# Attention probabilities and the residual turned by VectorE blocks and DMA instead of TensorE transposes

## The chip, the cores and the metric

One core of one Trainium2 chip runs the kernel. The time is the device time of one execution in microseconds (us), the median of the runs shown. TensorE (PE in the profile) multiplies matrices into eight accumulator banks; VectorE (DVE) and ScalarE (ACT) do the elementwise work, GpSimd (POOL) nearly nothing here. SyncE (SP) issues all the DMAs that this text speaks of, from one queue of its own.

## What is computed

Two layers of a transformer over 512 tokens of width 1,024, in float32: a state-space mixer (SSD), then latent attention (MLA) with 16 heads, each mixer behind a root-mean-square norm and added to the residual `h`, and a last norm. The change lies in the second layer. Cut to that:

```python
def mla_mixer(u, positions, in_w, q_norm_w, kv_norm_w, uq_w, ukv_w, out_w):
    proj = u @ in_w                                   # c_q 384, c_kv 256, k_r 64, z 2048
    q = rms_norm(c_q, q_norm_w) @ uq_w                # 16 heads x (128 + 64)
    kv = rms_norm(c_kv, kv_norm_w) @ ukv_w            # 16 heads x (128 + 128): k_nope, v
    q_full = [q_nope, rope(q_rope)]; k_full = [k_nope, rope(k_r)]
    o = causal_block_attention(q_full, k_full, v, 192 ** -0.5)
    return (o * silu(z)) @ out_w

def attend(qb, bi):                                   # a block of 128 queries
    s = einsum('bqhd,bkhd->bhqk', qb, k) * scale
    s = where(key_pos <= q_pos, s, -inf)
    return einsum('bhqk,bkhd->bqhd', softmax(s), v)
...
h = h + mla_mixer(rms_norm(h, norm_w[1]), ...)
return rms_norm(h, final_norm_w)
```

## The kernel before

**Precision.** A float32 operand is split in an upper half (ScalarE casts it to the matmul's float32 form) and a lower half (VectorE subtracts that from the operand), and each product is three matmul passes: upper by upper, upper by lower, lower by upper. So each weight and each activation costs a ScalarE cast and a VectorE subtraction before TensorE can use it. `split_weight` does it for weights (L272 and L273), `split` for activations (L311, L312). `weight()` keeps one unit split ahead of the one in use and one more loaded: loads go into 2 buffers (`raw`), halves into 3 (`whi`, `wlo`). `gemm` (L291) is a projection; it yields every six matmuls, so that other work can be placed between.

**Orders.** TensorE runs its instructions in the order in which the code is written. The order on the other engines, and that of SP's DMAs, is made by the scheduler of the framework from the same program; each engine then runs its list strictly from front to back.

**Stages.** The SSD layer lasts until about 415 us. Then come six projections of the MLA layer (U_M1, 24 matmuls each). In between, the residual, held as eight tiles of 128 channels by 512 tokens, is turned to tokens by channels: 32 TensorE transposes (L682), four to a bank, eight ScalarE copies and eight DMAs (L686) into a DRAM tile `hd`, from which the output projection reads it back at the end. Then come the norms, the first head's projections, and the head loop (L886 to L905), which runs from about 510 to 777 us:

- An even turn of the loop (h even) projects for head h+2, from weight `ua`: first the rope part of q for heads h+2 and h+3, rotated in `rope` (L687 to L701) with the help of four DMAs that swap row groups (L697), three VectorE passes (L698 to L700), and split into `s1` and `s2` (L736 to L739); then q (split by L311, L312) and k (L721 to L723) of head h+2.
- An odd turn projects q and k of head h+2 from weight `ub`, and the values of heads h+1 and h+2 from `uc` (L774).
- Each of the first eleven turns adds one projection of the gate (`zgemm`, weight `w`, result `z` at L712); later ones have pieces of the output projection (`out_tok`).

Into this feed go the steps of the attention, placed by hand-written tables of shares of the turn's cost: SC for `score(h+1, b)`, TU for `turn(h, kb)`, PR for `product(h, kb)`; SF places the scores of head 0 ahead of the loop.

- `score` (L794 to L799): block b of 128 queries against 128 (b+1) keys; then mask and maximum in one VectorE pass (L806; block 0 has a pass more, L804), the exponential on ScalarE (L223), reciprocal (L808) and scaling (L809) on VectorE. The probabilities `p` stand with queries on the partitions.
- `turn` (L818): TensorE transposes, 10 a head, bring them to keys on the partitions in a bank `pt`; ScalarE's cast makes `ph` (L822), VectorE's subtraction `pl` (L823).
- `product` (L836): three matmuls per key block into `po`; after the last, VectorE multiplies by the gate (L838).

A loop turn h thus holds the projections for head h+2, the scores of head h+1, and the transposes and products of head h. What the prediction calls an even head is an even turn of this loop.

Of the kernel before, what the change touches and what calls it, by code (L numbers as in the profile page):

```python
# [15 lines left out]
P = 128  # L16
T = 512
# [22 lines left out]
P1 = (1.0, 2.4, 3.8, 12.0, 18.2)  # L40
GN = 16.84
G7 = 33.0
SF = (0.02, 0.1, 2.1, 3.1)
SC = (0.0, 0.16, 0.25, 0.44)
TU = (0.02, 0.08, 0.38, 0.55)
PR = (0.3, 0.48, 0.65, 0.94)
KO = (3, 4, 5, 8, 10)
# [104 lines left out]
class Net:  # L152
# [497 lines left out]
    def mla(self):  # L650
# [5 lines left out]
        nc.sync.dma_start(con[:], t["con"][:, K_MASK:])  # L656
        self.mask, self.cosT, self.sinT = con[:, 0:T], con[:, T:2 * T], con[:, 2 * T:3 * T]
        hd = self.dram.tile([NCH, P, D], F32, name="hd")
        vh, vl = [], []
        for k in range(KD):  # L660
            h = self.h[k]
# [8 lines left out]
        for i in range(6):  # L670
            w = self.weight("w", U_M1 + i)
            ps = self.bank("mm")
            self.run(self.gemm(ps[:], w, vh, vl, KD))
            if i == NU:
                pss = self.sumsq([h[:] for h in self.h], D, "b")
                r1 = self.rstd_of(pss, D)
            if i >= 2:
                c = i - 2
                for n in range(2):
                    pt = self.bank("pt")  # L680
                    for k in range(4):
                        nc.tensor.transpose(pt[:, k * P:(k + 1) * P], self.h[4 * n + k][:, c * P:(c + 1) * P],  # L682
                                            self.ident)
                    ht = wk.tile([P, T], F32, tag=("ph", "pl")[n], name=self.nm("ht"))
                    nc.scalar.copy(ht[:], pt[:])
                    nc.sync.dma_start(hd[c, :, n * T:(n + 1) * T], ht[:])  # L686
            pend.append(ps)  # L687
            while pend and i >= NU:
                o = self.o16.tile([P, T], F32, tag="o", name=self.nm("cq"))
                v.tensor_tensor(o[:], pend.pop(0)[:], r1[:], op=ALU.mult)  # L690
                cq.append(o)
# [87 lines left out]
                f["v"].append((va, vb))  # L779
                yield 1.3  # L780

        probs = [[] for _ in range(MH)]

        def score(h, b):
            f, i = F[h // 2], h % 2
# [21 lines left out]
            self.E(p[:], p[:], AF.Exp, scale=-1.0, bias=st[:, 0:1], accum_out=st[:, 1:2])  # L807
            v.reciprocal(st[:, 2:3], st[:, 1:2])  # L808
            v.tensor_scalar(p[:], p[:], st[:, 2:3], None, op0=ALU.mult)  # L809
            probs[h].append(p)  # L810

        parts, acc = [[] for _ in range(MH)], {}

        def turn(h, kb):
            n = T - kb * P
            pt = self.bank("pt")
            for b in range(kb, NCH):
                nc.tensor.transpose(pt[:, (b - kb) * P:(b - kb + 1) * P], probs[h][b][:, kb * P:(kb + 1) * P],  # L818
                                    self.ident)
            ph = wk.tile([P, T], F32R, tag="ph", name=self.nm("ph"))  # L820
            pl = wk.tile([P, T], F32R, tag="pl", name=self.nm("pl"))
            nc.scalar.copy(ph[:, :n], pt[:, :n])  # L822
            v.tensor_tensor(pl[:, :n], pt[:, :n], ph[:, :n].bitcast(F32), op=ALU.subtract)  # L823
            parts[h].append((ph, pl))

        def product(h, kb):
# [20 lines left out]
            yield from self.out_tok(zt, 0, hd)  # L847

        def norm(tiles, n, cw):
            at = (wk, ("qh", "ql", "s2") if n == KVL else ("ph", "pl", "s2"))  # L850
            pss = self.sumsq([x[:] for x in tiles], n, "b", *at)
            r = self.rstd_of(pss, n, *at)
            hs, ls = [], []
            for i, x in enumerate(tiles):
                v.scalar_tensor_tensor(x[:], x[:], col(cw + i), r[:], op0=ALU.mult, op1=ALU.mult)
                a = wk.tile([P, T], F32R, tag="ch", name=self.nm("ch"), bufs=5)
                b = wk.tile([P, T], F32R, tag="cl", name=self.nm("cl"), bufs=5)
                nc.scalar.copy(a[:], x[:])
                v.tensor_tensor(b[:], x[:], a[:].bitcast(F32), op=ALU.subtract)
                hs.append(a)  # L860
                ls.append(b)
            return hs, ls

        outg = out0()
        self.run(zgemm(0))
# [15 lines left out]
        self.run(zgemm(3))  # L881
        zsilu(0)
        self.run(fa)
        self.run(front_b(0))
        self.sched(zgemm(4), [(x, functools.partial(score, 0, b)) for b, x in enumerate(SF)])
        for h in range(MH):  # L886
            if h and h % 4 == 0:
                zsilu(h // 4)
            feed, cost = [], 0.0
            j = h // 2 + 1  # L890
            if h < 14:
                feed.append(front_a(j) if h % 2 == 0 else front_b(j))
                cost += 5.2 if h % 2 == 0 else 5.9
            if h < 11:
                feed.append(zgemm(5 + h))
                cost += 5.2
            if h >= 11:
                k = KO[h - 11]
                feed.append(itertools.islice(outg, k))
                cost += 1.3 * k  # L900
            at = SC if h + 1 < MH else ()
            pieces = [(x * cost, functools.partial(score, h + 1, b)) for b, x in enumerate(at)]
            pieces += [(x * cost, functools.partial(turn, h, b)) for b, x in enumerate(TU)]
            pieces += [(x * cost, functools.partial(product, h, b)) for b, x in enumerate(PR)]
            self.sched(chain(*feed), pieces)  # L905
# [166 lines left out]
```

## Time and profile before

| | before |
|---|---|
| median of the runs | 840.74 us (840.42, 840.74, 841.0) |
| the profiled execution's own time | 840.15 us |
| its span, first to last instruction | 838.3 us |
| TensorE's granted clock over the span | 0.998 |
| TensorE busy (weight loads beside it) | 822.8 us, 98% (694.8) |
| VectorE / ScalarE / GpSimd busy | 640.2 (76%) / 453.5 (54%) / 0.2 us |
| DRAM read / written | 83.12 / 4.33 MB |

The profile's busy row gives each engine's busy time, its share of the span and its instructions; PEld is TensorE's loading of weights, which overlaps its matmuls. The chain of waits goes back from the last instruction to what released it, and names the share of the span that each engine holds. A row of it has the start, the length, and the engine, tile and line; "x9" is nine instructions in a row. A row of a group has the line, engine, operation, output and inputs with their shapes, and the count; then busy us and the mean ns of one; then the idle time just ahead of them and what ended it. An arrow `<-` after a number names what ended a wait. Line numbers are those of the kernel before, unless the kernel after is named; there, lines behind the residual's block stand one to fifteen off.

### The profile page before, as it was taken

To read this page: it belongs to the slowest core of one execution; us is meant where nothing else is said; L and a number is where in the kernel's file an instruction comes from. 1 tells how busy PE (TensorE), PEld (TensorE's weight loads), DVE (VectorE), ACT (ScalarE), POOL (GpSimd) and SP (SyncE) were. 2 spreads that over 40 slices of the span, in tenths; PEclk is the share of its full clock that TensorE was granted. 3 is DMA by queue.
4 is the path that set the end of the run, shared out by engine and by line. 5 is a ranking of instruction groups with operands and counts; after the bars stand their busy time and mean duration, and the time that the engine had idled before them with its cause. 6 is when DMAs were issued, how large, how long until landed. Compare 5 with 4: busy or idle time off the path is not lost.

```text
span 838.3 us, 11586 instructions
## 1 busy us (share of the span) xinstructions
PE 822.8 (98%) x4260; PEld 694.8 (83%) x4260; DVE 640.2 (76%) x1226; ACT 453.5 (54%) x802; POOL 0.2 (0%) x4
## 2 busy tenths in 40 slices
PE   7999999999999999999999999999999999999996
PEld 5887888888888888888888888888888888888885
DVE  7899898979788979776564887786767869675544
ACT  7567755545565657333354664456547557554233
POOL 0000000000000000000000000000000000000000
PEclk9999999999999999999999999999999999999999
DMA  6354543434242424323225242222221224331212
GB/s 227 102 186 145 153 150 106 147 101 128 98 151 76 151 87 137 121 95 101 90 86 176 79 129 64 77 65 73 73 64 56 89 75 157 100 100 53 92 59 100
DMA packets 35112, 90.55 MB, mean 108 GB/s; under 512 B 4784, under 2 KB 6320, under 8 KB 35056
## 3 DMA queue, kind: packets, MB, share of 16 engines
q1 hardware_dynamic: 34336, 88.77, 32.9%
q10 hardware_dynamic: 720, 1.05, 0.3%
q8 instruction: 33, 0.54, 0.3%
q14 instruction: 23, 0.19, 0.1%
HBM read 83.12 MB, written 4.33 MB: 104 GB/s over the span
## 4 chain that ended last, share of the span: by engine, by line
PE 91%; DVE 5%; DMA 2%; ACT 1%; issue 1%; SPq 0%; DVEq 0%; ACTq 0%
PE mm L291 54%; PE ot L942 11%; PE s L794 5%; PE mm L300 4%; PE po L836 4%; PE mm L774 3%; PE pt L818 2%; PE yd L138 2%; PE yd L291 1%; PE aux L130 1%; PE aux L105 1%; DMA x<-in_x_dram 1%; PE aux L77 1%; PE aux L89 1%; DMA L<-ac_d 1%; DVE wlo L273 1%
## 5 line engine op out<-in xcount | busy, mean ns | idle before, releaser
L272 ACT CAST whi<-raw 128x1024 fp32r<-128x1024 f32 (+3 forms) x132 | 127.0, 965 | 214.7 <-PE mm L291 177.4
L273 DVE TENSOR_TENSOR wlo<-raw,whi 128x1024 fp32r<-128x1024 f32 (+3 forms) x132 | 146.8, 1115 | 56.1 <-ACT whi L272 55.8
L291 PE MATMUL mm<-ah,whi 128*128 128x512 f32 x384 | 153.9, 401 | 0.0
L291 PE MATMUL mm<-ah,wlo 128*128 128x512 f32 x384 | 150.1, 391 | 0.4 <-DVE wlo L273 0.4
L291 PE MATMUL mm<-al,whi 128*128 128x512 f32 x384 | 149.8, 390 | 0.0
L291 PE MATMUL mm<-vh,whi 128*128 128x512 f32 x224 | 89.6, 400 | 0.9 <-ACT whi L272 0.9
L291 PE MATMUL mm<-vh,wlo 128*128 128x512 f32 x224 | 87.8, 392 | 0.7 <-DVE wlo L273 0.7
L291 PE MATMUL mm<-vl,whi 128*128 128x512 f32 x224 | 87.5, 391 | 0.0
L291 PEld LDWEIGHTS mm<-ah,wlo 128*128 128x128 f32 x384 | 72.1, 188 | 16.0 <-DVE wlo L273 0.8
L291 PEld LDWEIGHTS mm<-ah,whi 128*128 128x128 f32 x384 | 72.2, 188 | 15.5 <-issue 1.4
L291 PEld LDWEIGHTS mm<-al,whi 128*128 128x128 f32 x384 | 72.2, 188 | 14.4 <-DVE al L312 0.3
L942 PE MATMUL ot<-whi,ah 128*128 128x512 f32 (+1 forms) x136 | 52.3, 384 | 0.0
L942 PE MATMUL ot<-whi,al 128*128 128x512 f32 (+1 forms) x136 | 51.4, 378 | 0.0
L942 PE MATMUL ot<-wlo,ah 128*128 128x512 f32 (+1 forms) x136 | 51.4, 378 | 0.0
L291 PEld LDWEIGHTS mm<-vh,wlo 128*128 128x128 f32 x224 | 42.0, 188 | 10.8 <-DVE wlo L273 1.5
L291 PEld LDWEIGHTS mm<-vh,whi 128*128 128x128 f32 x224 | 42.1, 188 | 9.2 <-ACT whi L272 1.1
L223 ACT ACTIVATE p<-p,st 128x128 f32<-128x128 f32 (+1 forms) x64 | 36.1, 564 | 25.1 <-DVE st L806 25.0
L291 PEld LDWEIGHTS mm<-vl,whi 128*128 128x128 f32 x224 | 42.2, 188 | 7.2
L822 ACT CAST ph<-pt 128x512 fp32r<-128x512 f32 (+1 forms) x64 | 26.5, 422 | 33.2 <-PE pt L818 32.8
L291 PE MATMUL mm<-ch,whi 128*128 128x512 f32 x104 | 42.6, 409 | 0.0
L291 PE MATMUL mm<-ch,wlo 128*128 128x512 f32 x104 | 40.8, 392 | 0.0
L291 PE MATMUL mm<-cl,whi 128*128 128x512 f32 x104 | 40.7, 392 | 0.0
(225 smaller groups left out, 1642.6 us busy)
## 6 DMA issues: line engine op xcount, KB each, us to landing
raw<-in_w_dram SPq DMA_DIRECT2D x100, 512.0 KB, 3.3
L<-ac_d SPq DMA_DIRECT2D x32, 256.0 KB, 3.8
E<-ea_d SPq DMA_DIRECT2D x32, 128.0 KB, 3.3
raw<-in_ua_dram SPq DMA_DIRECT2D x8, 512.0 KB, 3.3
raw<-in_ub_dram SPq DMA_DIRECT2D x8, 320.0 KB, 2.9
x<-in_x_dram SPq DMA_DIRECT2D x8, 256.0 KB, 4.3
res<-in_x_dram SPq DMA_DIRECT2D x8, 256.0 KB, 3.3
hd<-ht SPq DMA_DIRECT2D x8, 256.0 KB, 2.3
```

The source lines that it names most:

```text
L138: nc.tensor.matmul(yd[64 * h:64 * h + 64, s], self.xdt[j][:, c, h, :], self.L[2 * j + h][:, s], start=True, stop=True)
L223: i = self.nc.scalar.activation(out, in_, func, **k)
L272: nc.scalar.copy(hi[:, a:b], raw[:, a:b])
L273: nc.vector.tensor_tensor(lo[:, a:b], raw[:, a:b], hi[:, a:b].bitcast(F32), op=ALU.subtract)
L291: self.nc.tensor.matmul(ps, a, b, start=i == 0, stop=i == len(seq) - 1)
L300: self.nc.tensor.matmul(p, seq[i][0], seq[i][1], start=i == 0, stop=i == 3 * ks - 1)
L774: nc.tensor.matmul(ps[:, c2 * 256:(c2 + 1) * 256], a, b, start=i == 0, stop=i == 5)
L794: nc.tensor.matmul(ps[:, :n], x[:, s], y[:, :n], start=k == 0, stop=k == 4)
L818: nc.tensor.transpose(pt[:, (b - kb) * P:(b - kb + 1) * P], probs[h][b][:, kb * P:(kb + 1) * P], self.ident)
L822: nc.scalar.copy(ph[:, :n], pt[:, :n])
L836: nc.tensor.matmul(po[:, kb * P:], x, y, start=kb == 0 and k == 0, stop=kb == NCH - 1 and k == 2)
L942: nc.tensor.matmul(ps[:, a:b], x, y, start=start and i == 0, stop=stop and i == 5)
```

## The change

Both transposes leave TensorE.

- *Residual.* VectorE's `transpose`, which turns each 32x32 block in its place, is applied to each of the eight residual tiles (two in each of the last four of the six projections; L681 of the kernel after); four DMAs a tile (L684), one for each group of 32 partitions, put the blocks in their turned places in `hd`, in runs of 32 numbers (128 bytes).
- *Probabilities.* At the end of each `score`, VectorE turns the 32x32 blocks of `p` into a tile `pb` (L810; two buffers), and four DMAs on SP (L814) write them to a DRAM tile `pd`, one for even and one for odd heads, again in runs of 128 bytes. A new piece, `fetch(h)`, stands right behind the four scores of the head, as the fifth entry of SC and SF: four DMAs (L830) read the key blocks back, whole rows, into tiles `pl`: for even heads four tiles of their own, for odd heads four tiles (`sqa`, `r0`, `rt`, `sq`) that the norms also use. So a head's reads stand behind its sixteen writes on SP.
- `turn` has no TensorE work left: ScalarE casts `ph` from `pl` (L837), VectorE subtracts in place (L838).
- The tables SF and SC have new numbers, and the scores of head 0 are spread over its own projections (`front_b(0)`) and one gate projection, where they stood in the gate projection only. The norm of q takes other tiles for its scratch.

```diff
--- before.py
+++ after.py
@@ -40,8 +40,8 @@
 G7 = 33.0
-SF = (0.02, 0.1, 2.1, 3.1)
-SC = (0.0, 0.16, 0.25, 0.44)
+SF = (0.6, 1.0, 2.0, 3.2, 8.0)
+SC = (0.0, 0.12, 0.2, 0.32, 0.55)
 TU = (0.02, 0.08, 0.38, 0.55)
@@ -656,6 +656,7 @@
         hd = self.dram.tile([NCH, P, D], F32, name="hd")
+        turned = hd[:].rearrange("c (j a) d -> a (c j) d", a=32)
         vh, vl = [], []
@@ -675,15 +676,13 @@
             if i >= 2:
-                c = i - 2
-                for n in range(2):
-                    pt = self.bank("pt")
-                    for k in range(4):
-                        nc.tensor.transpose(pt[:, k * P:(k + 1) * P], self.h[4 * n + k][:, c * P:(c + 1) * P],
-                                            self.ident)
-                    ht = wk.tile([P, T], F32, tag=("ph", "pl")[n], name=self.nm("ht"))
-                    nc.scalar.copy(ht[:], pt[:])
-                    nc.sync.dma_start(hd[c, :, n * T:(n + 1) * T], ht[:])
+                for k in (2 * i - 4, 2 * i - 3):
+                    ht = wk.tile([P, T], F32, tag="ph", name=self.nm("ht"))
+                    v.transpose(ht[:], self.h[k][:])
+                    for b in range(4):
+                        m = slice(32 * b, 32 * b + 32)
+                        nc.sync.dma_start(turned[:, :, k * P + 32 * b:k * P + 32 * b + 32],
+                                          ht[m, :].rearrange("a (j b) -> a j b", b=32))
             pend.append(ps)
@@ -779,7 +778,7 @@
 
-        probs = [[] for _ in range(MH)]
+        pd = [self.dram.tile([T, T], F32, name=f"pd{i}") for i in range(2)]
 
@@ -807,20 +806,36 @@
             v.tensor_scalar(p[:], p[:], st[:, 2:3], None, op0=ALU.mult)
-            probs[h].append(p)
+            pb = wk.tile([P, T], F32, tag="pb", name=self.nm("pb"))
+            v.transpose(pb[:, :n], p[:])
+            turned = pd[h % 2][:].rearrange("(j a) q -> a j q", a=32)
+            for i in range(4):
+                q = b * P + 32 * i
+                nc.sync.dma_start(turned[:, :n // 32, q:q + 32],
+                                  pb[32 * i:32 * i + 32, :n].rearrange("a (j q) -> a j q", q=32))
 
         parts, acc = [[] for _ in range(MH)], {}
+
+        back = {}
+
+        def fetch(h):
+            for kb in range(NCH):
+                n = T - kb * P
+                if h % 2:
+                    g = ("sqa", "r0", "rt", "sq")[kb]
+                    pl = self.nrm.tile([P, T], F32R, tag=g, name=self.nm("pl"), bufs=SQ if g == "sq" else 1)
+                else:
+                    pl = wk.tile([P, n], F32R, tag=f"pl{kb}", name=self.nm("pl"), bufs=1)
+                pl = pl[:, :n]
+                nc.sync.dma_start(pl.bitcast(F32), pd[h % 2][kb * P:(kb + 1) * P, kb * P:])
+                back[h, kb] = pl
 
         def turn(h, kb):
             n = T - kb * P
-            pt = self.bank("pt")
-            for b in range(kb, NCH):
-                nc.tensor.transpose(pt[:, (b - kb) * P:(b - kb + 1) * P], probs[h][b][:, kb * P:(kb + 1) * P],
-                                    self.ident)
+            pl = back[h, kb]
             ph = wk.tile([P, T], F32R, tag="ph", name=self.nm("ph"))
-            pl = wk.tile([P, T], F32R, tag="pl", name=self.nm("pl"))
-            nc.scalar.copy(ph[:, :n], pt[:, :n])
-            v.tensor_tensor(pl[:, :n], pt[:, :n], ph[:, :n].bitcast(F32), op=ALU.subtract)
+            nc.scalar.copy(ph[:, :n], pl.bitcast(F32))
+            v.tensor_tensor(pl, pl.bitcast(F32), ph[:, :n].bitcast(F32), op=ALU.subtract)
             parts[h].append((ph, pl))
@@ -847,7 +862,7 @@
         def norm(tiles, n, cw):
-            at = (wk, ("qh", "ql", "s2") if n == KVL else ("ph", "pl", "s2"))
+            at = (wk, ("qh", "ql", "s2"))
             pss = self.sumsq([x[:] for x in tiles], n, "b", *at)
@@ -860,6 +875,9 @@
             return hs, ls
+
+        def steps(h):
+            return [functools.partial(score, h, b) for b in range(NCH)] + [functools.partial(fetch, h)]
 
@@ -881,8 +899,7 @@
         self.run(fa)
-        self.run(front_b(0))
-        self.sched(zgemm(4), [(x, functools.partial(score, 0, b)) for b, x in enumerate(SF)])
+        self.sched(chain(front_b(0), zgemm(4)), list(zip(SF, steps(0))))
         for h in range(MH):
@@ -899,7 +916,7 @@
             at = SC if h + 1 < MH else ()
-            pieces = [(x * cost, functools.partial(score, h + 1, b)) for b, x in enumerate(at)]
+            pieces = [(x * cost, fn) for x, fn in zip(at, steps(h + 1))]
             pieces += [(x * cost, functools.partial(turn, h, b)) for b, x in enumerate(TU)]
```

How the change moves the other engines' lists is seen at the places below. The rows are taken from the two programs in the order in which each engine runs them; a row has the line, the operation and its output and inputs with their numbers.

**VectorE where an odd turn ends and an even one begins (head 2).** `raw` 4864 before and 4903 after are the same weight, `ua` of that head, which its first projection reads; `wlo` is its lower half, `z` out of `mm` the gate's projection (the last of the odd turn), `z` out of `po` the product of the head that ends, and `p` of shape 128x128 the first block of the new scores. Before:

```order
L273 TENSOR_TENSOR wlo_4933<-raw_4864,whi_4932 128x1024
L723 TENSOR_TENSOR k_4837<-mm_4830,k_4837 128x512
L808 RECIPROCAL st_4847<-st_4847 128x1
...
L809 TENSOR_SCALAR p_4921<-p_4921,st_4922 128x512
L712 TENSOR_TENSOR z_4970<-mm_4936,rr_3966 128x512
L273 TENSOR_TENSOR wlo_5098<-raw_4976,whi_5097 128x640
L838 TENSOR_TENSOR z_4278<-po_4887,z_4278 128x512
L804 TENSOR_TENSOR p_4993<-s_4989,con_3835 128x128
```

After:

```order
L777 TENSOR_TENSOR vb_4962<-mm_4948,va_4961 128x512
L810 STREAM_TRANSPOSE pb_4942<-p_4936 128x512
L711 TENSOR_TENSOR z_5016<-mm_4977,rr_3966 128x512
L853 TENSOR_TENSOR z_4264<-po_4926,z_4264 128x512
L273 TENSOR_TENSOR wlo_4974<-raw_4903,whi_4973 128x1024
L803 TENSOR_TENSOR p_5039<-s_5035,con_3835 128x128
```

Before, the lower half of the new head's weight is made some seventeen rows ahead of the old turn's last `z`, and what stands at the boundary is the weight for the turn after (`wlo` 5098, 640 wide). After, the new head's weight itself stands at the boundary, behind both `z`.

**VectorE where the rotation of head 2 is made and where that even turn ends.** `rraw` and `rsw` are the rope part of q and its swapped copy, whose third pass gives the rotated q; the passes on 64 partitions make the lower halves that the scores of the next turn read as `s1` and `s2`; `raw` 5095 before and 5162 after is the value weight `uc`. Before, in the middle of the even turn:

```order
L312 TENSOR_TENSOR ql_5071<-mm_5036,qh_5070 128x512
L273 TENSOR_TENSOR wlo_5159<-raw_5095,whi_5158 128x512
L698 TENSOR_TENSOR rraw_5020<-rraw_5020,con_3835 128x512
L699 TENSOR_TENSOR rsw_5022<-rsw_5022,con_3835 128x512
L723 TENSOR_TENSOR k_5081<-mm_5074,k_5081 128x512
L700 TENSOR_TENSOR rraw_5020<-rraw_5020,rsw_5022 128x512
...
L738 TENSOR_TENSOR s_984_5030<-rraw_5020,s_984_5030 64x512
L739 TENSOR_TENSOR s_985_5031<-rraw_5020,s_985_5031 64x512
```

After, at the turn's end (ahead of "...") and in the odd turn that follows:

```order
L810 STREAM_TRANSPOSE pb_5153<-p_5147 128x512
L711 TENSOR_TENSOR z_5210<-mm_5168,rr_3966 128x512
L697 TENSOR_TENSOR rraw_5079<-rraw_5079,con_3835 128x512
L698 TENSOR_TENSOR rsw_5081<-rsw_5081,con_3835 128x512
L853 TENSOR_TENSOR z_4329<-po_5137,z_4329 128x512
L699 TENSOR_TENSOR rraw_5079<-rraw_5079,rsw_5081 128x512
L737 TENSOR_TENSOR s_985_5089<-rraw_5079,s_985_5089 64x512
L738 TENSOR_TENSOR s_986_5090<-rraw_5079,s_986_5090 64x512
...
L808 TENSOR_SCALAR p_5293<-p_5293,st_5294 128x384
L810 STREAM_TRANSPOSE pb_5271<-p_5265 128x256
L273 TENSOR_TENSOR wlo_5219<-raw_5162,whi_5218 128x512
```

The rotation moved from the middle of the even turn to its end, behind the gate's `z`, and the value weight from the middle of the even turn to the odd turn, behind the softmax of block 2.

**ScalarE in an even turn, at the first casts of probabilities (head 2).** `ph` is the cast that the products read, 512 wide for key block 0; `p` of 256 and 384 columns are the exponentials of the next head's blocks 1 and 2, `whi` a weight's upper half, `qh` the upper half of q. Before:

```order
L272 CAST whi_5097<-raw_4976 128x640
L822 CAST ph_5005<-pt_5000 128x512
L223 ACTIVATE p_4993,st_4994<-p_4993,st_4994 128x128
L822 CAST ph_5013<-pt_5009 128x384
L732 COPY rraw_5020<-mm_4982 128x512
L223 ACTIVATE p_5049,st_5050<-p_5049,st_5050 128x256
```

After:

```order
L731 COPY rraw_5079<-mm_5028 128x512
L223 ACTIVATE p_5108,st_5109<-p_5108,st_5109 128x384
L272 CAST whi_5024<-raw_4971 128x1024
L311 CAST qh_5123<-mm_5095 128x512
L837 CAST ph_5052<-pl_4984 128x512
L837 CAST ph_5055<-pl_4986 128x384
```

The first two casts moved from ahead of the next head's block 1 to behind its block 2, a weight's upper half and `qh`.

## The prediction

> **What bounds the kernel now.** First the page: its busy row and, in the chain that ended last, the shares by engine.
>
> ```profile
> span 838.3 us, 11586 instructions
> PE 822.8 (98%) x4260; PEld 694.8 (83%) x4260; DVE 640.2 (76%) x1226; ACT 453.5 (54%) x802; POOL 0.2 (0%) x4
> PE 91%; DVE 5%; DMA 2%; ACT 1%; issue 1%; SPq 0%; DVEq 0%; ACTq 0%
> ```
>
> TensorE sets the end. Next the table by windows, for 200 us of the head loop (length, then busy us of PE, PEld, DVE, ACT, POOL, clock, DMA share, GB/s), and for the first 20 us, needed later:
>
> ```profile
> 500.00:700.00 200.00, 200.00 (x1090) 173.79 (x1089) 149.66 (x367) 111.46 (x239) 0.00 (x0) 1.00 0.24 76
> 0.00:20.00 20.00, 14.04 (x51) 10.66 (x51) 14.06 (x29) 15.50 (x28) 0.20 (x4) 1.00 0.71 237
> ```
>
> TensorE never pauses there, so whatever it stops doing is gained and whatever it waits for is lost. Then the chain in order of time, an even and an odd head (start, us, what), and one row of the residual's turn:
>
> ```profile
> 443.03 0.87 PE pt L682 x8
> ...
> 541.07 1.43 PE mm L291 x6
> ...
> 542.84 0.76 PE pt L818 x7
> 543.60 2.08 PE mm L291 x9
> 545.68 1.47 PE s L794 x10
> 547.14 2.08 PE mm L291 x9
> 549.22 0.69 PE po L836 x3
> 549.91 0.22 PE pt L818 x2
> ...
> 558.08 1.43 PE mm L291 x6
> 559.50 0.12 PE s L797
> 559.62 0.06 PE s L798
> 559.68 0.17 PE s L799
> 559.85 0.76 PE pt L818 x7
> 560.62 2.09 PE mm L291 x9
> 562.71 1.48 PE s L794 x10
> 564.18 1.43 PE mm L774 x12
> ...
> 575.90 1.43 PE mm L291 x6
> ```
>
> An even head takes 17.0 us (541.07 to 558.08), an odd one 17.8, a pair 34.8. A transpose costs the chain 0.109 us (0.87 / 8; 0.76 / 7).
>
> **What it removes.** 160 transposes of probabilities and 32 of the residual, 192 x 0.109 = 20.9 us, all on the path: 1.1 us of each head, 3.5 us ahead of the loop. ScalarE loses eight copies that nobody waits for.
>
> **What it adds in work.** VectorE turns four blocks a head, 1,280 columns, and eight residual tiles. No row shows a 32x32 turn. The nearest are VectorE's one-input and two-input passes over the same tiles, at 384 columns (mean ns after the comma):
>
> ```profile
> L809 DVE TENSOR_SCALAR p<-p,st 128x384 f32<-128x384 f32 x12 | 5.1, 421 | 0.4
> L823 DVE TENSOR_TENSOR pl<-pt,ph 128x384 fp32r<-128x384 f32 x11 | 6.1, 554 | 0.0
> L823 DVE TENSOR_TENSOR pl<-pt,ph 128x256 fp32r<-128x256 f32 x11 | 4.6, 416 | 0.0
> ```
>
> I take the dearer, a turn being no scaling by one number: 0.28 to 0.69 a block, 1.9 us a head (1.5 by the cheaper, which would take under 0.1 from any wait below). VectorE is 75% busy in the loop (149.7 of 200), 13 us of a 17.4 us head; with 1.9 more it still fits. So its load does not decide; its order does. The eight residual tiles, 5 us of VectorE and 24 more DMAs on SP, lie under six projections of 24 matmuls at 0.23 us, 33 us, in which each weight is loaded and split one projection ahead: no term.
>
> **What it moves: four places where TensorE now waits.** TensorE's order is written out, the other engines' is the scheduler's, and every engine runs strictly in order. In the orders above, four results that used to be made half a head early now stand directly ahead of their use. I lay each place out with durations of these groups:
>
> ```profile
> L272 ACT CAST whi<-raw 128x1024 fp32r<-128x1024 f32 x16 | 16.8, 1050 | 18.5 <-PE mm L291 13.8 <-PE mm L774 4.7
> L273 DVE TENSOR_TENSOR wlo<-raw,whi 128x512 fp32r<-128x512 f32 x6 | 4.2, 692 | 0.3 <-ACT whi L272 0.3
> L806 DVE CUSTOM_DVE_ANT_0 p<-s,con 128x384 f32<-128x384 f32 x12 | 6.6, 550 | 2.6 <-PE s L794 2.6
> L223 ACT ACTIVATE p<-p,st 128x384 f32<-128x384 f32 x12 | 7.4, 618 | 3.5 <-DVE st L806 3.5
> L808 DVE RECIPROCAL st<-st 128x1 f32<-128x1 f32 x48 | 7.6, 159 | 6.4 <-ACT p L223 6.3
> L311 ACT CAST qh<-mm 128x512 fp32r<-128x512 f32 x11 | 6.4, 581 | 0.0
> L822 ACT CAST ph<-pt 128x512 fp32r<-128x512 f32 x12 | 7.0, 588 | 17.6 <-PE pt L818 17.6
> L736 ACT CAST s<-rraw 64x512 fp32r<-64x512 f32 x6 | 3.7, 621 | 11.9 <-DVE rraw L700 11.9
> ```
>
> and with VectorE's timeline at a head's boundary (start, duration):
>
> ```profile
> 557.83 0.69 DVE L712 TENSOR_TENSOR z<-mm,rr 128x512 f32<-128x512 f32 x1 [1.90 <-PE mm L291]
> 558.44 0.68 DVE L838 TENSOR_TENSOR z<-po,z 128x512 f32<-128x512 f32 x1
> 559.04 1.21 DVE L273 TENSOR_TENSOR wlo<-raw,whi 128x1024 fp32r<-128x1024 f32 x1
> ```
>
> VectorE starts a 512-wide pass every 0.61 us; it reaches `z` only when the head's last projection ends, 0.25 us ahead of the boundary at 558.08.
>
> *Place 1, the q weight, even head.* The after order at an even head's start is this very row of three, except that the third is now the weight of the head that begins. It ends at 560.25, 2.2 us past the boundary; TensorE's third matmul, the first to read it, would start 0.4 us past it (two of 1.43 / 6, less a little overlap). Wait 1.8, say 1.9 with the hop between engines. Heads 2 to 14, seven times: 13.3 us.
>
> *Place 2, the probabilities, even head.* `ph` of head h now follows, on ScalarE, the exponential of the next head's block 2, a weight's upper half and `qh`. From block 2's last matmul: reduction 0.55, exponential and its sum 0.7, weight 1.0, `qh` 0.5, `ph` 0.6, hops 0.1: 3.4 us. TensorE has only nine projection matmuls ahead of the product, 2.08, which it leaves 0.15 before their end: wait 1.5. Then `pl` follows a weight's lower half on VectorE and comes 0.4 later than the third matmul wants it. Together 1.9; head 0 has 2.9 (two more casts stand ahead), head 12 has 1.0 (no weight): 5 x 1.9 + 3.9 = 13.4.
>
> *Place 3, the rotation, odd head.* After the late `z` come two passes of the rotation, the product's `z` and the third pass: 4 x 0.61 - 0.25 = 2.2 us past the boundary for its start, 2.9 for its end, 3.5 with ScalarE's cast (0.62), 4.3 with VectorE's half. TensorE wants it for the third matmul of block 0, 1.4 us past (559.68 less the 0.2 by which a matmul starts before the one ahead of it ends). Wait 2.9. Head 1 has the rotation ahead of `z` (0.2), head 11 two splits more (3.3), head 13 no `z` (2.6): 4 x 2.9 + 6.1 = 17.7.
>
> *Place 4, the value weight, odd head.* Its lower half stands behind block 2's softmax and block 1's turn, while TensorE goes from block 2 straight to it (562.71, then 564.18). Reduction 0.55, exponential and sum 0.7, reciprocal 0.16, scaling 0.4, turn 0.4, weight 0.69, hops 0.2: 3.1 us. Seven heads, and 0.5 for head 11: 22.2.
>
> The same chains stand in the tail: the output weight behind head 12's last softmax 2.0; in head 14 `ph` behind two weights of 1.0 each, 3.7; the last head's fetch 1.5; ahead of the loop, block 0 of head 0 right behind its `k`, 0.9. Together 8.1.
>
> **SP's queue.** Sixteen writes, four reads a head. Issue times (min/median/max ns) of the nearest rows and a wide load's landing:
>
> ```profile
> L686 SPq DMA_DIRECT2D hd<-ht x8: 319/324/601, 444.8 to 464.1; - x8
> L697 SPq DMA_DIRECT2D rsw<-rraw x32: 507/586/792, 483.0 to 719.9; - x32
> raw<-in_ua_dram SPq DMA_DIRECT2D x8, 512.0 KB, 3.3
> ```
>
> No row shows a DMA in runs of 128 bytes. I take 0.6 us, the 32-partition row, being nearest in shape. A pair of heads then holds SP 32 x 0.6 + 8 x 0.32 + 5 x 0.33 + 4 x 0.59 = 26 us of 42. The reads add a wait for a head's last writes; the next head's writes and weights queue behind it, and ScalarE's casts wait for those. Counted on from the places above: block 3's turn ends 17 us into an even head, its writes are issued by 19.5 and land by 23, the reads 3 us later, 6 us into the odd head, where place 4 lets `ph` start at 12; in the other parity the reads stand behind a weight that waits for place 1's split (2.2 us in), land by 7, and place 2 lets `ph` start at 10. The turn adds a wait too: its two buffers make VectorE, with reductions and splits queued behind, wait for the writes of two blocks before; they land 2.7 us or more ahead of it. So no term at 0.32 or 0.6. At 1.0 the q weight, behind four writes, comes 1 us later, 7 us in all. By share, 0.24 at 76 GB/s means 317 GB/s at full share; 1.3 MB more a head is 4 us of engine time beside 4.2 of 17.4. That fits even at double.
>
> [...]
>
> **The sum.** 13.3 + 13.4 + 17.7 + 22.2 + 8.1 = 74.7 us of waits, less 20.9: +53.8, on the profiled execution's 840.15 (span 838.3 and 1.85 around it) 894 us. That execution lies 0.6 under the median of 840.74, inside the runs' spread. A regular pair goes from 34.8 to 42.4.
>
> **Rivals.** *SP becomes the bound.* From (42.4 - 6.6) / 32 = 1.1 us a write its queue sets the pace, weights come late for good; at 1.5 us a pair takes 54.6, 12 more, seven times: 978. For it: runs this short are in no row; against it: every issue in the two rows above is under 0.8. Chance 0.2. *The waits don't come.* If the orders hold enough slack after all, only the removal is left: 840.15 - 20.9 = 819. For it: TensorE waits for nothing between 500 and 700 now; against it: each of the four chains starts at a matmul directly ahead of the waiting one, so an idle VectorE doesn't shorten it. 0.05. *Half of it.* Places 1 and 2 hidden and the rest two thirds: 32 - 20.9, 851, and with luck no change: 0.05. *The clock falls.* Waits of 3 us at seven places could lower TensorE's granted clock behind them. Against it: its longest wait now
>
> ```profile
> PE mm L300 <- ACT whi L272: 4.8, 1, 4.8
> ```
>
> lies in the first 20 us, whose window has 1.00. If the 4 us behind places 3 and 4 ran at half speed, 14 x 2 = 28 more: 922. 0.08. [...]
>
> My forecast has 0.62. The range reaches from two thirds of the waits (50 - 20.9: 869) to writes of 1.37 us on SP (a pair of 50.4, 8 more, seven times: 950), and holds the clock's case. Runs tell 0.2%, 1.7 us, apart: faster 0.06, same 0.04, slower 0.90.
>
> **What would show it.** Right: TensorE's waits name `wlo` (line 273) at two places a pair, `s` (737) and `ph` (837), 1.5 to 3.5 us each, about 75 in all; PE busy under 810 in a longer span; pairs of about 42 us. Wrong: pairs of 33 us; or SP issues over 1 us with `raw` DMAs as the releasers; or a clock under 1.00 in the loop.

## The result and the profile after

The changed kernel takes 916.54 us (median of four runs, 913.38 to 922.75), the kernel before 840.67 in the same comparison: 1.091 times as long, with a 95% interval of 1.085 to 1.097. The forecast was 894, with a range of 869 to 950. Its profiled execution took 916.87 us, its span is 915.1. First its page, as above: the span, the busy row, the chain's shares.

```profile
span 915.1 us, 11824 instructions
PE 836.2 (91%) x4068; PEld 690.6 (75%) x4068; DVE 677.7 (74%) x1298; ACT 450.7 (49%) x794; POOL 0.2 (0%) x4
PE 71%; DVE 14%; DMA 6%; issue 4%; ACT 3%; SPq 2%; DVEq 0%; ACTq 0%
```

TensorE has 192 instructions fewer and is busy for 13.4 us more. The 200 us of the head loop that were shown of before now read:

```profile
500.00:700.00 200.00, 167.71 (x777) 137.30 (x776) 132.32 (x314) 85.83 (x183) 0.00 (x0) 0.94 0.47 113
```

TensorE pauses for 32.3 of 200 us, no other engine is near its limit, and the granted clock is 0.94. Its pauses by what ended them (us in total, times, longest), the kernel after:

```profile
PE s L798 <- DVE s L737: 16.7, 7, 3.3
PE mm L773 <- ACT whi L272: 15.3, 7, 3.3
PE po L851 <- ACT ph L837: 11.5, 9, 2.6
PE mm L291 <- DVE wlo L273: 6.9, 9, 1.1
...
PE mm L291 <- ACT whi L272: 4.5, 7, 1.7
PE mm L773 <- DVE wlo L273: 4.4, 7, 0.7
PE ot L959 <- DVE wlo L273: 1.9, 2, 1.4
PE po L851 <- DVE pl L838: 1.6, 3, 0.6
PE ot L959 <- ACT whi L272: 1.2, 1, 1.2
```

These are the four places by name: the rotation (737), the value weight (773), the probabilities (837, 838), the q weight (291). The chain in an odd turn shows the third and the fourth (the longest pieces):

```profile
565.11 0.68 DVE rraw L697
565.78 0.60 DVE rsw L698
566.39 0.60 DVE z L853
566.99 0.61 DVE rraw L699
567.62 0.63 ACT s L735
568.27 0.70 DVE s L737
569.01 0.39 PE s L798
...
570.70 2.56 PE mm L291 x6
...
574.55 0.56 DVE p L805
...
576.43 0.43 DVE pb L810
576.86 0.58 DVE wlo L273
577.49 2.71 PE mm L773 x11
```

The steps are those of the prediction. But six projection matmuls take 2.56 us where the chain of before had 1.43. The table by windows, one microsecond each, says why (the clock is the third number from the end; the next window has 0.50 too):

```profile
571.00:572.00 1.00, 1.00 (x4) 0.80 (x3) 1.00 (x5) 0.36 (x3) 0.00 (x0) 0.50 0.00 0
```

Behind the pause of 2.67 us that ends at 569.01 the granted clock is 0.50. In windows of half a microsecond the loop has eleven stretches of half clock, eight of 3.4 us and three of 6.8. That is fourteen lengths of 3.4 us, each losing 1.7: 24 us. The mean clock gives the same: (1 - 0.972) x 915.1 less (1 - 0.998) x 838.3 is 23.9.

So the 76.8 us of span are made up as follows. TensorE's pauses grew from 15.5 (838.3 - 822.8) to 78.9 (915.1 - 836.2), by 63.4. Its work fell by 20.9 and grew by at most 23.9 of slow clock, a little of which falls into pauses; 10.4 or somewhat more are left over. Those I put, by estimate, to restarts: a 512-wide matmul counts 0.39 to 0.50 us by itself and 0.23 in a row, and there are some 50 pauses. No run takes the restarts apart.

### The profile page after: what moved, and what is told of

Read it like the earlier page. It is cut to its first block, busy times and chain, and to the rows that moved or that the text cites. A ratio compares the mean times of both kernels' runs of the same rounds, so it can differ in the third digit from the quotient of the medians.

```text
span 915.1 us, 11824 instructions
## 1 busy us (share of the span) xinstructions
PE 836.2 (91%) x4068; PEld 690.6 (75%) x4068; DVE 677.7 (74%) x1298; ACT 450.7 (49%) x794; POOL 0.2 (0%) x4
## 4 chain that ended last, share of the span: by engine, by line
PE 71%; DVE 14%; DMA 6%; issue 4%; ACT 3%; SPq 2%; DVEq 0%; ACTq 0%
PE mm L291 42%; PE ot L959 8%; PE s L793 4%; PE mm L300 3%; PE mm L773 3%; DVE wlo L273 2%; PE po L851 2%; PE yd L138 2%; DMA pd<-pb 2%; SPq L814 1%; PE yd L291 1%; PE aux L130 1%; ACT whi L272 1%; DVE pb L810 1%; DMA raw<-in_w_dram 1%
## 5 line engine op out<-in xcount | busy, mean ns | idle before, releaser
L291 PEld LDWEIGHTS mm<-ah,whi 128*128 128x128 f32 x384 | 72.2, 188 | 15.3 <-issue 1.4
L291 PE MATMUL mm<-ch,wlo 128*128 128x512 f32 x104 | 43.6, 420 | 5.5 <-DVE wlo L273 5.5
L291 PE MATMUL mm<-cl,whi 128*128 128x512 f32 x104 | 42.6, 410 | 0.0
L805 DVE CUSTOM_DVE_ANT_0 p<-s,con 128x256 f32<-128x256 f32 (+2 forms) x48 | 26.6, 554 | 18.5 <-PE s L793 18.0
```

Of the source, the lines that this page charges most:

```text
L291: self.nc.tensor.matmul(ps, a, b, start=i == 0, stop=i == len(seq) - 1)
L805: v.tensor_tensor_reduce(p[:], ps[:, :n], mask, -SCALE, 3.0e38, ALU.add, ALU.min, st[:, 0:1])
```

## Experiments

The theory after the result: SP's queue, which now carries 20 short transfers a head, makes the scheduler expect the weights and row swaps late, so that it lists what needs them late on VectorE and ScalarE; those lists, not the transfers, make TensorE wait, and the waits halve the clock. What the scheduler expects is inferred; the runs show only its lists. Rivals: the round trip of the probabilities through DRAM is what is late; or the transfers on SP are. Each run stands beside runs of the kernel before on the same chip (840.3 to 840.7 us); the ratio is to those. Unless said otherwise the edit is to the changed kernel.

**The residual's part alone.** The edit takes that part of the diff into the kernel before.

> The residual's part alone, probabilities still turned by TensorE. Theory (its 24 more writes and VectorE's 8 turns lie under six long projections): 32 transposes of 0.109 us less, 3.5 us, so 837.2 us (836.5 to 838). Rival (its short-run writes hold up the weight loads on SP as those of the probabilities do): 840 or more, with new waits of TensorE on a weight between 440 and 470 us.

836.26 us, ratio 0.995 (0.9937 to 0.9962): 4.0 us less, 3.2 to 5.3 by the interval, where 3.5 were expected. TensorE has no new wait. This part is a gain, and the run is faster than both kernels; what follows is the probabilities'.

**The same traffic, used by nobody.** TensorE's transposes make `ph` and `pl` again; the reads go into four tiles of the norms in all heads.

```diff
+            probs[h].append(p)
...
-            pl = back[h, kb]
+            pt = self.bank("pt")
+            for b in range(kb, NCH):
+                nc.tensor.transpose(pt[:, (b - kb) * P:(b - kb + 1) * P], probs[h][b][:, kb * P:(kb + 1) * P],
+                                    self.ident)
```

> The changed kernel, but TensorE turns the probabilities again as before and the products use those; VectorE's turns, the writes and the reads stay, and nobody uses what is read. So nothing waits for the round trip, and SP's queue carries all of it. Theory (what shares SP's queue is listed late): the waits for the q weight, the rotation and the value weight stay (about 46 us with 20 us or more of slow clock behind them), place 2 goes, 17.4 us of transposes come back: 915 us (900 to 930). Rival (the round trip, as the two runs with GpSimd's queue suggest): no dependence, no wait: 836.3 of the run with the residual's part alone and a little more, 836 to 845.

920.18 us, ratio 1.094 (1.092 to 1.096). TensorE's waits in it:

```profile
PE s L799 <- DVE s L737: 20.6, 7, 3.5
PE mm L773 <- ACT whi L272: 16.1, 7, 2.4
PE mm L291 <- DVE wlo L273: 9.6, 9, 1.7
```

Nothing in this kernel depends on the round trip, and three of the four places wait as before; only `ph` is gone. This speaks against the round trip as the cause in the changed kernel. The run keeps the new tables and VectorE's turns beside the traffic on SP, so it doesn't tell these apart; two of the runs with later products, below, do.

**The lists alone.** Every DMA stays where it is on SP and TensorE's order is the same; the scheduler is told to put some instructions behind others on their own engine.

```diff
-            v.tensor_tensor(z[:], ps[:], r1[:], op=ALU.mult)
+            with tc.issue_after(self.rot.ins) if i >= 5 and i % 2 else ExitStack():
+                v.tensor_tensor(z[:], ps[:], r1[:], op=ALU.mult)
...
+            with ExitStack() as late:
+                if h % 2 == 0 and h and b == 2:
+                    for x in self.uc:
+                        late.enter_context(tc.issue_after(x.ins))
```

> The changed kernel with every DMA where it was on SP, in the same order, and TensorE's order unchanged; only VectorE's and ScalarE's lists are mended at two places: in even turns both multiplications into z stand behind the rotation's third pass, and in odd turns block 2's reduction, exponential and reciprocal stand behind both halves of the value weight. Theory (the lists make TensorE wait, not the transfers, which landed 6 us or more ahead of use there): the rotation's wait goes (17 us), the value weight's falls from 2.6 to about 1 us a turn (12 us less), and 11 stretches of halved clock at 1.7 us with them: 868 us (858 to 885). Rival (on SP behind the writes the transfers themselves are late): the waits stay and name a DMA; 895 or more.

890.04 us, ratio 1.060 (1.056 to 1.063), 26.5 less than the changed kernel. The same rows:

```profile
PE mm L291 <- DVE wlo L273: 8.9, 9, 1.7
PE mm L775 <- DVE wlo L273: 5.2, 7, 0.7
...
PE s L800 <- DVE s L738: 4.4, 6, 3.3
PE mm L775 <- ACT whi L272: 4.3, 6, 1.4
```

The rotation's wait fell from 16.7 to 4.4 us, the value weight's from 19.7 (15.3 + 4.4) to 9.5, close to the expected zero and 7; no transfer was touched. So at these two places the lists make TensorE wait. Of the 22 us by which the time missed 868, some 10 are waits: all of TensorE's pauses together fell by 19.5 us (78.9 to 59.4), where 29 were expected. Some 10 are the clock, which came back by 9 us only (0.972 to 0.981, (1 - 0.981) x 888.7 = 16.9 for 25.6), where 19 were expected: stretches now follow the pauses for the q weight (0.6 and 0.9 us close together, or 1.7) in three of the six turns that have them, where the changed kernel had one of six.

**The clock alone.**

```diff
+            if b == 0 and h % 2 == 0 and h:
+                for _ in range(12):
+                    nc.tensor.matmul(ps[:, 2 * P:], kh[0][:, s], kh[0][:, :2 * P], start=True, stop=True)
...
+                if half == 0 and j:
+                    for _ in range(12):
+                        nc.tensor.matmul(ps[:, :2 * P], kh[0][:, :P], kh[0][:, :2 * P], start=True, stop=True)
```

> The changed kernel with twelve needless matmuls of 256 columns (1.4 us together, results overwritten or never read) placed on TensorE at each of the two longest waits of a pair of heads, ahead of the instruction that waits, so that its pause falls from 2.7 to about 1.2 us; no other engine's list moves. Theory (TensorE's clock halves for 3.4 us behind a pause of over 2 us and not behind one of 1.2): the granted clock goes from 0.972 to 0.99 or more, and 14 stretches x 1.7 us are saved: 892 us (885 to 899). Rival (the clock falls for another cause, such as DMA traffic or the mix of work): 916, the clock stays at 0.97.

907.27 us, ratio 1.082 (1.079 to 1.085), 9 less with 168 matmuls more; the clock rose to 0.989. The loop's lengths of half clock fell from fourteen to five, all behind the longest remaining pauses (1.9 and 0.5 together, 2.9, 2.6), none behind the shortened ones. So the pause brings the slow clock, not the traffic, which was the same. The expected 892 took all fourteen for these two places; eleven were, and part of the time went back into other waits.

**Two queues: the weight loads, then the row swaps too, on GpSimd's.**

```diff
-        self.nc.sync.dma_start(raw[:], self.t[kind][idx])
+        (self.nc.gpsimd if idx >= U_MZ or kind != "w" else self.nc.sync).dma_start(raw[:], self.t[kind][idx])
...
-                nc.sync.dma_start(sw[32 * i:32 * i + 32, :], raw[32 * j:32 * j + 32, :])
+                nc.gpsimd.dma_start(sw[32 * i:32 * i + 32, :], raw[32 * j:32 * j + 32, :])
```

> The changed kernel with the MLA layer's weight loads (gate, q, k and value weights, output weights) issued by GpSimd on its own queue; writes, reads and the rotation's row swaps stay on SP. Theory (SP's queue: the scheduler lists the results that wait for a load behind the writes): the waits for the q weight (9.5 us) and the value weight (19.7) and the slow clock behind the latter (12) go, those of the rotation (16.7, line 737 or 738) and of ph (13) stay: 875 us (862 to 885). Rival 1 (the round trip of the probabilities through DRAM is what is late): 905 or more, ph the largest wait. Rival 2 (loads issued by GpSimd come later still): 916 or more.

> As the run with the weight loads on GpSimd's queue, and the rotation's four row swaps there too, so that SP holds the probabilities' writes and reads alone. Theory (SP's queue): the wait for the rotation goes as well with the slow clock behind it, 29 us more; ph still waits, 13 to 20 us: 843 us (832 to 855). Rival 1 (the round trip): 905 or more. Rival 2 (GpSimd's issue is slow): 916 or more.

895.98 us (ratio 1.067, 1.063 to 1.070) with the first line alone, 896.14 (1.067, 1.064 to 1.069) with both. The waits did what the theory says. With the first alone:

```profile
PE po L851 <- ACT ph L837: 31.2, 10, 4.2
PE s L798 <- DVE s L737: 19.0, 6, 3.3
```

The waits for the q weight and the value weight are gone, the rotation's stays. With both lines the rotation's is gone as well, but:

```profile
PE po L851 <- ACT ph L837: 42.1, 14, 5.3
PE po L851 <- DVE pl L838: 6.6, 6, 3.2
```

The time hardly moved, because a wait that the others had covered took their place. The chain of the second run shows what it is:

```profile
574.76 2.59 DMA pl<-pd
577.42 0.63 ACT ph L837
578.10 1.23 PE po L851 x3
```

Now it is the round trip: the reads are issued at 574.76, 3.3 us before the product. Part of that trip is again the queue's order, since the reads stand on SP behind three writes of the next head's first block, issued from 573.05, while the last write of their own head had landed by 570.25. So the first rival is wrong for the changed kernel and right for the one in which the queue is mended. I had priced that wait at 13 to 20 us.

**Later products.** The next runs give the trip more time: the products move from 0.3, 0.48, 0.65 and 0.94 of a turn to 0.55, 0.68, 0.8 and 0.94, first in the changed kernel itself, then with loads and swaps on GpSimd's queue, then with the writes and reads there instead. The cut shows what the three share.

```diff
-PR = (0.3, 0.48, 0.65, 0.94)
+PR = (0.55, 0.68, 0.8, 0.94)
```

> The changed kernel with the later products alone, all DMAs on SP as in the change. Theory: the waits for ph and pl go (13 us), those for the q weight, the rotation and the value weight stay with their slow clock: 903 us (895 to 909). Rival (the late fetch is the root and holds the others): below 870.

> As the run with weight loads and row swaps on GpSimd's queue, and the products placed later in TensorE's order, at 0.55, 0.68, 0.8 and 0.94 of a turn in place of 0.3, 0.48, 0.65 and 0.94: about 4.3 us more for the fetched probabilities. Theory (there only the round trip is late, by up to 5.3 us, mostly 2 to 4): the 49 us of waits for ph and pl go and 24 us of slow clock with them: 823 us (816 to 835), below both kernels. Rival (the trip grows with what it may take, or a later wait moves in): 850 or more.

> The changed kernel with later products, and the other half of the queue moved: the probabilities' writes and reads are issued by GpSimd, weights and row swaps stay on SP. Theory (it only matters that they don't share a queue): as the run with the loads on GpSimd, 823 us (816 to 838). Rival (GpSimd takes longer to issue one in short runs: a load took it 0.54 us in the runs before; 20 a head are 11 of 17 us, so that the round trip is late again): 850 or more, ph the largest wait.

906.06 us (ratio 1.078, 1.074 to 1.082) for the first: the waits for `ph` and `pl` are gone but for 0.2 us, the other three stay, as the theory had it. 874.42 (1.040, 1.038 to 1.042) for the second, 22 less than without, and 866.03 (1.031, 1.029 to 1.032) for the third; not the 823 expected of both: `ph` and `pl` still cost 31.2 and 27.9 us. The first and the third differ only in the queue of the writes and reads, and in the third the waits for the q weight, the rotation and the value weight are gone. So these three come from sharing SP's queue; the tables and VectorE's turns, the same in both, don't make them by themselves. GpSimd's queue in the third run shows one reason for what is left (start, length, what):

```profile
575.90 2.58 POOL L814 DMA_DIRECT2D pd<-pb  x4 [1.30 <-DVE pb L810]
584.27 1.65 POOL L814 DMA_DIRECT2D pd<-pb  x3 [5.79 <-DVE st L807]
...
587.38 2.20 POOL L830 DMA_DIRECT2D pl<-pd  x4
```

A head's last writes end at 578.5; its reads stand behind the next head's first four writes, which wait for that head's first softmax, and go out 8.9 us later. That place is the smaller reason: for some 12 of the 21.4 us of waits for `ph` in this run the trace has the read landed 0.6 to 3 us before ScalarE starts the cast, which stands in its list behind other passes, mostly the next head's exponentials or the gate's.

**The reads ahead of those writes.** First by giving the reads to SP, then by a single DRAM tile for all heads, then with the products of even turns later still.

```diff
-                nc.gpsimd.dma_start(pl.bitcast(F32), pd[h % 2][kb * P:(kb + 1) * P, kb * P:])
+                nc.sync.dma_start(pl.bitcast(F32), pd[h % 2][kb * P:(kb + 1) * P, kb * P:])
...
-        pd = [self.dram.tile([T, T], F32, name=f"pd{i}") for i in range(2)]
+        pd = [self.dram.tile([T, T], F32, name="pd0")] * 2
...
+PRE = (0.74, 0.82, 0.9, 0.97)
-            pieces += [(x * cost, functools.partial(product, h, b)) for b, x in enumerate(PR)]
+            pieces += [(x * cost, functools.partial(product, h, b)) for b, x in enumerate(PR if h % 2 else PRE)]
```

> Later products, the probabilities' writes on GpSimd's queue, and their reads on SP with the weights and row swaps. In the run with both on GpSimd a head's reads were listed behind the next head's first four writes and so issued some 6 us after the last write of their own had landed; here no write stands ahead of them. Theory (that place in the queue is what is left of the late ph and pl): their 28 us of waits and 8.5 us of slow clock go: 830 us (820 to 842), about 10 below the kernel before. Rival (the trip itself is too long for 0.55 of a turn, or ScalarE's and VectorE's lists hold ph back without it): 855 or more.

> Later products, writes and reads on GpSimd's queue, and one DRAM tile for all heads in place of two, so that a head's reads must stand ahead of the next head's writes, which now wait for them. Theory (the reads' place): ph and pl wait less, but the turn of block 3 moves behind the turn's last multiplication by z on VectorE, which takes back some of it: 838 us (825 to 852). Rival (the reads' place doesn't matter, or the new wait costs as much): 860 or more.

> As the run with the writes on GpSimd's queue, the reads on SP and later products, and in even turns the products later still, at 0.74, 0.82, 0.9 and 0.97: some 2.8 us more where that run still waits 2.7 + 0.45 us in each of five turns, and 2.8 in the first. Theory (only the distance between scores and products is short there): 18 us of waits and some 10 us of slow clock go: 832 us (826 to 842), no slower than the kernel before. Rival (the four products, pressed together with two buffers of ph, wait for each other's casts, or the lists move again): 850 or more.

859.75 us (ratio 1.023, 1.021 to 1.024), 886.38 (1.055, 1.053 to 1.057) and 857.23 (1.019, 1.017 to 1.021): all three missed. In the first the regular odd turns don't wait any more, five even ones still wait 3.2 us. There the reads stand on SP behind the load of the q weight, which goes out only when the buffer that it fills is free:

```profile
551.67 0.33 SPq L263 DMA_DIRECT2D raw<-in_ua_dram  x1
552.31 1.75 SPq L830 DMA_DIRECT2D pl<-pd  x4
```

The head's last write had landed at 546.16. The first read lands at 556.17, and ScalarE, busy until then with block 3's exponential and the rotation's two casts, starts `ph` at 556.40: its list adds 0.2 us. The reads had got rid of the writes ahead of them and got a weight load instead.

In the second VectorE's list has the last block's turn behind the turn's multiplications by `z`, as expected. But half of its 35.0 us of waits for `ph` are three of 5.9 us, for which the reads had landed 3 to 5 us before the cast: ScalarE's list has the gate's passes (L232) and their table loads of 1.28 us ahead of it. So the run doesn't tell what the reads' place is worth. In the third the wait changed into many small ones:

```profile
PE po L852 <- ACT ph L838: 15.1, 14, 4.4
PE po L852 <- DVE pl L839: 7.6, 13, 1.0
```

22.7 us where the first of the three had 23.1; the clock alone is better (0.988 for 0.983). The best arrangement with the probabilities by DMA is still 16.5 us over the kernel before. Whether another order reaches the 820 us that the removal alone would give wasn't tried and stays open.

## Why the prediction was right, and where not

- *The removal, 20.9 us.* Right as far as it was tried apart: 4.0 for the residual's 32 transposes, 3.5 expected.
- *VectorE's turns, 0.28 to 0.69 us a block.* Right: 0.71 for the widest (709 ns in its row), 0.31 for the narrowest, 2.0 a head for the 1.9 taken.

```profile
L810 DVE STREAM_TRANSPOSE pb<-p 128x512 f32<-128x512 f32 x10 | 7.1, 709 | 0.2
```

- *The four places.* Right in cause, a little dear in size:

| | forecast, us | measured, us |
|---|---|---|
| 1, q weight | 13.3 | 9.5 (6.9 + 4.5, less 1.0 + 0.9 of before; in six turns, not seven) |
| 2, probabilities, with the tail's 3.7 + 1.5 | 18.6 | 13.1 (11.5 + 1.6) |
| 3, rotation | 17.7 | 16.7 |
| 4, value weight | 22.2 | 19.7 (15.3 + 4.4) |
| output weight, start of the loop | 2.9 | 3.9 (1.9 + 1.2, and 0.8) |
| sum | 74.7 | 62.9 |

At place 2 a regular even turn waits 1.24 us for `ph` and 0.1 for `pl`, where 1.9 were laid out for both. The list holds `ph` there, not the trip: in the turn of head 2 the first read goes out at 547.69 and lands at 550.80, and the cast starts at 554.90. At place 4 the longer part, 15.3 us, is for the upper half, which ScalarE makes behind block 2's exponential; the prediction named only the lower half, which ends the same chain.

- *SP's queue: "no term at 0.32 or 0.6".* Half right. A write took 0.45 us to issue, so SP did not become the bound and that rival (978 us, chance 0.2) is out. But its order did delay one transfer on the chip:

```profile
L814 SPq DMA_DIRECT2D pd<-pb x256: 302/449/784, 494.9 to 840.8; - x128
...
572.41 13.06 SPq L814 DMA_DIRECT2D pd<-pb  x12
585.57 0.41 SPq L263 DMA_DIRECT2D raw<-in_ua_dram  x1
...
ACT whi L272 <- DMA raw<-in_ua_dram: 15.7, 6, 4.9
```

Twelve writes hold SP for 13 us, because each block's four wait for its turn on VectorE, and the q weight's load stands behind them. So at place 1 the first part of the wait, for `whi` (4.5 us), is a late transfer. What I counted was the issue time of the writes, not what they wait for.

- *The clock.* This is the step that failed: the forecast had no term for it, and its rival gave "14 x 2 = 28 more: 922" a chance of 0.08. It measured 23.9 (14 x 1.7), and with the 10.4 us that are left over it outweighs the 11.8 us by which the waits were too dear: 53.8 - 11.8 + 23.9 + 10.4 = 76.3, of 76.8 measured. That 916.5 lies in the range is in part luck: two errors pull against each other, and the range's upper end was drawn for slow writes on SP, which didn't come.

I had set the rival aside for one row, the pause of 4.8 us in the first 20 us, whose window has a clock of 1.00. That was a misreading. The trace's record of the clock starts only at 9.19 us (at 10.75 in the kernel after), and the table counts time without a record as full speed. The matmuls, all 512 wide there, show that it was half (the kernel before; the count behind PE is the number of matmuls):

```profile
5.00:9.00 4.00, 4.00 (x10) 2.96 (x11) 2.87 (x7) 2.92 (x6) 0.00 (x0) 1.00 0.97 341
10.00:14.00 4.00, 4.00 (x19) 3.32 (x18) 4.00 (x9) 3.85 (x10) 0.00 (x0) 1.00 0.90 302
```

So a slow stretch does follow that pause. Whether the pause makes it or the start of the execution isn't told apart, but the row was no witness against the rival.

The traces also show why the same pause brings a slow stretch in some turns and not in others. In the kernel after, and by windows of half a microsecond in seven other runs, every change of the recorded clock lies a whole multiple of 3.413 us from every other, to 0.02 us (the stretches at 532.99, 570.53, 577.36 and 614.91 of the kernel after: 11, 2 and 11 lengths apart). In that kernel every full-speed length of this grid in which TensorE pauses for 1.87 us or more is followed by a slow one, and none with 1.78 or less; in the seven others the border lies between 1.5 and 1.9 (1.50 was followed by a slow one with the lists alone; 1.75 was not with later products and loads and swaps on GpSimd's queue). The pause of 2.67 us at 611.89 lies within one length, the same pause at 702.68 is cut into 0.97 and 1.70, and the clock stays at 1.00, in the length behind them too:

```profile
611.50:614.91 3.41, 0.74 (x5) 0.56 (x5) 2.69 (x5) 1.23 (x2) 0.00 (x0) 1.00 1.03 358
614.91:618.32 3.41, 3.41 (x13) 2.83 (x12) 2.38 (x10) 1.46 (x4) 0.00 (x0) 0.50 0.08 25
...
700.24:703.66 3.42, 2.44 (x14) 1.98 (x12) 2.82 (x5) 0.00 (x0) 0.00 (x0) 1.00 0.75 222
703.66:707.07 3.41, 1.72 (x10) 1.57 (x11) 2.23 (x6) 1.82 (x3) 0.00 (x0) 1.00 0.65 237
```

So the slow stretches of the loop are one or two lengths of a fixed grid, at a clock of 0.50. The rival spoke of waits of 3 us; 1.87 us of pause in one length of 3.41 was enough in the kernel after.

- *"PE busy under 810", "pairs of about 42".* Wrong by the same step and what is left over beside it: 836.2, and the q weight's wait ends at 547.14, then at 592.71 and 636.81 two turns later each, 45.6 and 44.1 us.

## What to carry to other kernels

When TensorE is the bound and its order is written out, price a change by the lists of the other engines: twenty more transfers on a queue that also loads weights moved results that no transfer of them touched, and the kernel with a copy that nobody read took 80 us more than the one before. Where a row of waits is found, look for the one that hides behind it, since ending the waits at three places, 46 us, gave 20 back. And give the pauses of TensorE a second price, here about 1.7 us where some 1.5 to 1.9 us of them fell into one length of 3.4, be it in one piece or two. Take parts of a change apart, as one of the two here was a gain of 4 us. A table's 1.00 for the clock is worth a look at the matmuls themselves where the record may have a gap.

## What the runs showed of the hardware

- Stretches of half clock (0.50), one or two lengths of 3.4 us, followed pauses of 2.67 us, of 1.9 and 0.7 close together, and in one run of 0.6 and 0.9; at other times the same pauses had none, as the grid of 3.413 us cut them. What counted in these runs was the pause within one length of the grid, from 1.5 to 1.9 us on.
- Writes of 64 KB in runs of 128 bytes took 1.9 us to land for the probabilities, about as the row swaps' 64 KB in whole rows (2.0), but 3.5 for the residual's.

```profile
pd<-pb SPq DMA_DIRECT2D x64, 64.0 KB, 1.9
hd<-ht SPq DMA_DIRECT2D x32, 64.0 KB, 3.5
```

- The share of the DMA engines in the loop doubled, 0.24 to 0.47, for 1.5 times the bytes (76 and 113 GB/s), so that the added traffic took engine time out of proportion. Reads and writes weren't told apart, and no wait is seen to come of it.
